# Elementwise work on on-chip data moves from GpSimd to VectorE and ScalarE in a two-block trunk kernel

## The chip, the cores and the metric

The kernel runs on one core of one Trainium2 chip. The metric is device time in microseconds (us). Engines go by the profile's names: PE is TensorE (PEld its weight load), DVE is VectorE, ACT is ScalarE, POOL is GpSimd, SP is SyncE, which here issues most DMAs.

## The reference, cut to what matters

Two blocks run one after the other over 512 latent tokens of 1024 features (the first block also over 256 context tokens). Everything is float32.

```python
# first block, twice: modulation, then three mixers side by side, then a squared-ReLU MLP
u = (rmsnorm(x, g_mix) * (1 + sc1) + sh1) @ w_in            # 1024 -> 2048 and some
mix = concat([pool_mixer(p), gla_output(gla_bidir(...)), latent_attention(q, k, v)]) @ w_out
x = x + ga1 * mix
x = x + ga2 * (square(relu(h @ w_up)) @ w_down)             # hidden width 4096
# second block, once: two recurrent scans side by side, gated and merged, then the same kind of MLP
u = (rmsnorm(x) * (1 + sc) + sh) @ w_in2                     # 1024 -> 14400
conv = silu(causal_depthwise_conv(u_part, w))                # 4 taps
y_gdn = gated_delta_rule(...)                                # 16 heads of 128
y_ssm = ssd_chunked_scan(...)                                # 32 heads of 64, state 128, chunks of 128
merged = sigmoid(g1) * (y_gdn_gated @ w_up1) + sigmoid(g2) * (y_ssm_gated @ w_up2)
x = x + norm(merged @ w_out2);  x = x + norm(mlp(...))
```

## The kernel before

**Products.** Every dense product is done with three float32r matmuls, `mm3`: an operand is split into a high part (rounded to float32r) and a low part (the rest), and high times high, high times low and low times high are added in PSUM. Weights come from DRAM in loads of 128 x 1024, "halves" in what follows: 512 rows and 256 columns. `whalf` (L274 to L287) loads one on SP's queue (L281, three buffers), makes the high part on ACT (L282, two buffers) and the low part by a subtraction that DVE and POOL share: `share` eighths of the columns on DVE (L284), the others on POOL (L285). `share` is 5, so 640 and 384 columns, and 4 between the scans and the merge, so 512 and 512. There are 503 halves. `dense` gives feature-major outputs of 512 tokens (48 matmuls for a half), `tokens` token-major ones (both halves of a group are needed until its end).

**What sets the order.** A scheduler orders the instructions of each engine when the kernel is built, from a simulated timeline; tiles and semaphores are placed by it. `urgent` pulls a weight's load and split and the use of its products ahead. Each engine then takes its instructions strictly in that order.

**First block.** `squares`, `root`, `spread` and `modulate` are the normalisation: squares on ACT, partial sums of them (L378) in turns on DVE and POOL, the power -0.5 of a few columns on POOL (L395). `gla_states` and `gla_out` are the gated linear attention: for each chunk of 128 tokens and each of seven levels, a difference E (L705, POOL), two exponentials (L706, L707, ACT), K (L708, DVE) and Q (L711 POOL, or L726 and L729: a memset on POOL, then half of the partitions on DVE and half on POOL), a product on PE and a masked copy (L734, DVE). `attend` is the softmax attention; its queries are scaled (L912) and turned (L836) on POOL. `mlp` squares the ReLU on POOL (L1051) between two ACT instructions (L1050, L259).

**Second block.** `conv_silu` takes a product's 512 columns: copy (L1283), last tap (L1285 or L1287) and first tap (L1288) on ACT, two taps on DVE (L1291), the first tap added on POOL (L1292), tanh on ACT, the last product on DVE (L1294). `gdn_prep`, `gdn_solve`, `gdn_join` and `gdn_chunk` are the delta rule, four chunks one behind the other; `ssm_chunk` is a chunk of a group of the state space scan (8 groups of 4 chunks), each with steps on PE, ACT, DVE and POOL. The dense products of `silu_tokens` and `sigmoid_gate` come behind the scans in the program, and the scheduler puts them between the scans' steps. `up` merges: its four parts need `gdn_gate` (two parts) and `ssm_gate` (two parts), whose first product is on POOL (L1779, L1800); L1830, L1832 and L1833 apply the gates. `post_norm` (L1260, L1261) adds the normalised output, every second block on POOL; it is the kernel's last step, before the stores.

Of the kernel before, what the change touches and what calls it, by code (L numbers as in the profile page):

```python
# [27 lines left out]
# ---------------------------------------------------------------- host side: layout and shape constants  # L28
# [43 lines left out]
def _bands():  # L72
    """Windowed mean minus the token itself, as matrices over [token in, token out]."""
# [118 lines left out]
# ---------------------------------------------------------------- the kernel  # L192
class Kern:
    SHARED = {"const", "wraw", "whi", "wlo", "mod", "gs", "nv", "nr"} | {f"V{i}" for i in range(8)}
    # work space: tag -> count, of [128, 512]
    WORK1 = dict(E=2, K=2, Q=2, AT=1, QE=1, q=2, d=1, ab=1)
    WORK2 = dict(fa=3, fr=2, fu=2, fy=2, gG=3, gk=2, gm=2, dv=2, dk=2, dq=2, da=2, dn=2, dd=2, jy=2)
    # the tags of a normalisation's square, variance, root and product
# [5 lines left out]
    def __init__(self, ctx, tc, A, at):  # L204
# [3 lines left out]
        self.share = 5  # L208
# [11 lines left out]
    def w(self, tag, n=512, dt=F32):  # L220
        """Work space [128, n]."""
# [21 lines left out]
    # -- small helpers  # L243
# [29 lines left out]
    # -- weights  # L273
    def whalf(self, name, i, n, kb, soon=True):  # L274
        """One load of a packed weight: its two float32r parts, [128, kb, n / kb]."""
# [23 lines left out]
    def dense(self, name, groups, h, n, consume, halves=(0, 1), soon=True):  # L299
        """out^T [128 features, n tokens] per block of 128 columns of the weight; h per block of its rows."""  # L300
# [15 lines left out]
    def tokens(self, name, g, h, ntb, consume):  # L316
        """out [128 tokens, 256] for pairs of token blocks."""
# [39 lines left out]
    def squares(self, x, n, tags, gains=None):  # L357
        """Means over the features of the squares of x, plus epsilon: token-major columns [128, n / 128]. With gains
        [128, 8, 2], as second columns the means of the squares times those."""
# [10 lines left out]
        for k in range(8):  # L370
# [6 lines left out]
            elif k > 1:  # L377
                (nc.gpsimd if k % 2 else nc.vector).tensor_tensor(accs[k % 2], accs[k % 2], sq, op=ALU.add)  # L378
# [8 lines left out]
        # EPS v + mean: the second norm's variance over the first one's factor  # L387
# [4 lines left out]
    def root(self, v):  # L392
        """v ** -0.5"""
# [4 lines left out]
    def spread(self, r):  # L398
        """Columns [128 tokens, blocks] as a row over all partitions, [128, tokens]."""
# [7 lines left out]
    def norm_mod(self, x, n, gs, sh, hs, tags):  # L407
        """hs: pairs that take the two parts of the normalised blocks."""
# [60 lines left out]
    def flush(self):  # L469
        """Ends the pieces that were begun."""  # L470
# [3 lines left out]
    def modulation_v(self, name, st, bias, part, first=0):  # L474
        """The same for the first condition alone, by the vector engine."""
# [20 lines left out]
    def tick(self, n=1):  # L496
        """Does the next pieces of what was left for later."""
# [6 lines left out]
    def gain(self, mod, j, g):  # L504
        """(1 + scale) * gain for condition j."""
# [17 lines left out]
    def after(self, a, tile):  # L523
        """Has the loads into a tile wait for an array: they would take the place of more urgent ones."""
# [1395 lines left out]
```

## Time and profile before

| | |
|---|---|
| three runs, median (lowest to highest) | 3656.49 us (3649.99 to 3657.73) |
| span of the profiled execution | 3646.2 us |
| PE busy, share | 3414.7 us, 94% |
| PE weight load | 2833.3 us, 78% |
| DVE busy, share | 2174.3 us, 60% |
| ACT busy, share | 1466.0 us, 40% |
| POOL busy, share | 1601.3 us, 44% (1370 instructions) |
| mean granted TensorE clock | 0.956 |
| DMA queues, of 16 engines | 38.3% and 3.5% |

The profiled execution's span is 10.3 us under the median of the runs: what lies around the span. A group of the page's costliest instructions gives its busy time, the mean of one, the idle time of the engine before them and what ended it. Ends of matmuls are modelled, so that PE counts as busy while a short matmul's result is still on its way.

### The profile page before, as it was taken

To read this page: it belongs to the slowest core of one execution; us is meant where nothing else is said; L and a number is where in the kernel's file an instruction comes from. 1 tells how busy PE (TensorE), PEld (TensorE's weight loads), DVE (VectorE), ACT (ScalarE), POOL (GpSimd) and SP (SyncE) were. 2 spreads that over 40 slices of the span, in tenths; PEclk is the share of its full clock that TensorE was granted. 3 is DMA by queue.
4 is the path that set the end of the run, shared out by engine and by line. 5 is a ranking of instruction groups with operands and counts; after the bars stand their busy time and mean duration, and the time that the engine had idled before them with its cause. 6 is when DMAs were issued, how large, how long until landed. Compare 5 with 4: busy or idle time off the path is not lost. (4 is left out here: it accounts for less than half of the span.)

```text
span 3646.2 us, 55656 instructions
## 1 busy us (share of the span) xinstructions
PE 3414.7 (94%) x20714; PEld 2833.3 (78%) x20714; DVE 2174.3 (60%) x3724; ACT 1466.0 (40%) x2587; POOL 1601.3 (44%) x1370
## 2 busy tenths in 40 slices
PE   7999999989999999999999998998899998989998
PEld 5777788877788787677788776787898776788886
DVE  4844877457533358755633789768757767564233
ACT  4522765453222255632223655554233323254222
POOL 2522465542343235422344555446445545555433
PEclk9898999999999999999999999999999999989999
DMA  6344124635522220045522364456366666454222
GB/s 224 116 143 137 44 74 140 213 117 162 174 99 98 94 70 22 10 134 189 188 95 91 120 195 131 153 159 191 124 186 203 196 201 184 144 167 145 94 97 75
DMA packets 268414, 492.67 MB, mean 135 GB/s; under 512 B 44912, under 2 KB 129904, under 8 KB 267888
## 3 DMA queue, kind: packets, MB, share of 16 engines
q1 hardware_dynamic: 214128, 447.17, 38.3%
q10 hardware_dynamic: 54016, 41.95, 3.5%
q8 instruction: 163, 2.67, 0.3%
q14 instruction: 107, 0.88, 0.1%
HBM read 431.22 MB, written 57.80 MB: 134 GB/s over the span
## 5 line engine op out<-in xcount | busy, mean ns | idle before, releaser
L285 POOL TENSOR_TENSOR wlo<-wraw,whi 128x384 fp32r<-128x384 f32 (+1 forms) x503 | 736.1, 1464 | 1265.2 <-ACT whi L282 1178.0
L295 PE MATMUL mm<-h,whi 128*128 128x512 f32 (+1 forms) x2344 | 865.3, 372 | 38.1 <-ACT h L418 7.4
L282 ACT ACTIVATE whi<-wraw 128x1024 fp32r<-128x1024 f32 x503 | 530.9, 1056 | 866.2 <-PE mm L296 648.2
L296 PE MATMUL mm<-h,whi 128*128 128x512 f32 (+1 forms) x2344 | 857.6, 366 | 14.2 <-DVE h L419 11.7
L284 DVE TENSOR_TENSOR wlo<-wraw,whi 128x640 fp32r<-128x640 f32 (+1 forms) x503 | 481.7, 958 | 636.3 <-ACT whi L282 629.8
L297 PE MATMUL mm<-h,wlo 128*128 128x512 f32 (+1 forms) x2344 | 841.0, 365 | 6.0 <-DVE wlo L284 5.9
L295 PEld LDWEIGHTS mm<-h,whi 128*128 128x128 f32 x2344 | 448.7, 192 | 124.2 <-ACT whi L282 11.5
L296 PEld LDWEIGHTS mm<-h,whi 128*128 128x128 f32 x2344 | 449.8, 192 | 93.4 <-DVE h L419 20.9
L297 PEld LDWEIGHTS mm<-h,wlo 128*128 128x128 f32 x2344 | 448.4, 192 | 80.7 <-DVE wlo L284 8.8
L296 PE MATMUL mm<-wlo,h 128*128 128x256 f32 x1200 | 353.5, 296 | 32.5 <-DVE wlo L284 27.7
L295 PE MATMUL mm<-whi,h 128*128 128x256 f32 x1200 | 353.2, 297 | 10.7 <-ACT whi L282 9.8
L297 PE MATMUL mm<-whi,h 128*128 128x256 f32 x1200 | 350.0, 293 | 0.0
L296 PEld LDWEIGHTS mm<-wlo,h 128*128 128x128 f32 x1200 | 235.2, 196 | 43.1 <-DVE wlo L284 32.5
L295 PEld LDWEIGHTS mm<-whi,h 128*128 128x128 f32 x1200 | 234.7, 197 | 27.7 <-ACT whi L282 12.5
L297 PEld LDWEIGHTS mm<-whi,h 128*128 128x128 f32 x1200 | 235.2, 196 | 17.2 <-issue 13.7
L295 PE MATMUL mm<-U,whi 128*128 128x512 f32 (+1 forms) x608 | 228.6, 379 | 5.8 <-DVE V L1080 5.8
L296 PE MATMUL mm<-U,whi 128*128 128x512 f32 (+1 forms) x608 | 227.5, 376 | 0.9 <-DVE U L260 0.9
L297 PE MATMUL mm<-U,wlo 128*128 128x512 f32 (+1 forms) x608 | 223.6, 376 | 0.0
L487 DVE SCALAR_TENSOR_TENSOR AT<-mraw,cst,AT 128x512 f32<-128x512 f32 x140 | 119.2, 851 | 88.6 <-DMA mraw<-in_w_ada 52.7
L295 PE MATMUL mm<-big,whi 128*128 128x512 f32 x384 | 155.0, 405 | 5.6 <-ACT whi L282 2.3
L296 PE MATMUL mm<-big,whi 128*128 128x512 f32 x384 | 153.6, 400 | 0.0
L297 PE MATMUL mm<-big,wlo 128*128 128x512 f32 x384 | 150.9, 401 | 0.0
(580 smaller groups left out, 5980.3 us busy)
## 6 DMA issues: line engine op xcount, KB each, us to landing
wraw<-in_w_in SPq DMA_DIRECT2D x166, 512.0 KB, 3.5
wraw<-in_w_up SPq DMA_DIRECT2D x96, 512.0 KB, 3.3
wraw<-in_w_down SPq DMA_DIRECT2D x96, 512.0 KB, 3.3
mraw<-in_w_mod SPq DMA_DIRECT2D x96, 256.0 KB, 3.0
mraw<-in_w_ada SPq DMA_DIRECT2D x96, 256.0 KB, 2.8
wraw<-in_w_out SPq DMA_DIRECT2D x40, 512.0 KB, 3.3
wraw<-in_w_mlp_up SPq DMA_DIRECT2D x40, 512.0 KB, 3.3
mraw<-in_w_late SPq DMA_DIRECT2D x64, 256.0 KB, 2.8
```

Of the source, the lines that this page charges most:

```text
L282: nc.scalar.activation(hi, raw, AF.Copy)
L284: nc.vector.tensor_tensor(lo[:, :c], raw[:, :c], hi[:, :c].bitcast(F32), op=ALU.subtract)
L285: nc.gpsimd.tensor_tensor(lo[:, c:], raw[:, c:], hi[:, c:].bitcast(F32), op=ALU.subtract)
L295: nc.tensor.matmul(out, lh, rh, start=start, stop=False)
L296: nc.tensor.matmul(out, lh, rl, start=False, stop=False)
L297: nc.tensor.matmul(out, ll, rh, start=False, stop=stop)
L487: nc.vector.scalar_tensor_tensor(acc, raw, st[:, k, 0:1], acc, op0=ALU.mult, op1=ALU.add)
```

## The change

- `whalf`: the low part is one DVE subtraction of 1024 columns; `share` is gone.
- `squares`, `gla_states`, `gla_out`, `turn`, the queries' scale, `first_norms`, `post_norm`, `ssm_chunk`, `ssm_gate`, `up`: the POOL instruction becomes a DVE one.
- `mlp`: the square is done by ACT.
- `conv_silu`: the first tap is a third DVE multiply-add; its ACT product and POOL addition are gone.
- `gdn_prep`: the two half subtractions become one DVE instruction of 512 columns; `gdn_chunk`: values are scaled by two ACT instructions, the two decays by one DVE instruction.
- `silu_tokens`: with a gain, ACT's halving and POOL's product become one DVE product with a gain that has been halved once.
- `ssm_chunk`: subtract and clip, two instructions of 512 columns, become four of 128 with both operations.
- `gdn_gate`: POOL's product and two DVE scalings become two DVE instructions.

POOL keeps the roots (L395, 15 of them), its memsets and its copies that hold back loads (L525): 107 rows in its order, where there were 1335. Comments are gone, and line numbers of the changed kernel are up to 7 lower.

```diff
 whalf:
-            c = (n * self.share // 8) // 64 * 64
-            nc.vector.tensor_tensor(lo[:, :c], raw[:, :c], hi[:, :c].bitcast(F32), op=ALU.subtract)
-            nc.gpsimd.tensor_tensor(lo[:, c:], raw[:, c:], hi[:, c:].bitcast(F32), op=ALU.subtract)
+            nc.vector.tensor_tensor(lo, raw, hi.bitcast(F32), op=ALU.subtract)
 squares:
-                (nc.gpsimd if k % 2 else nc.vector).tensor_tensor(accs[k % 2], accs[k % 2], sq, op=ALU.add)
+                nc.vector.tensor_tensor(accs[k % 2], accs[k % 2], sq, op=ALU.add)
 gla_out:
-                nc.gpsimd.tensor_tensor(v(E), v(B), v(B)[:, :, s:s + 1].to_broadcast([128, G, 2 * s]), op=ALU.subtract)
+                nc.vector.tensor_tensor(v(E), v(B), v(B)[:, :, s:s + 1].to_broadcast([128, G, 2 * s]), op=ALU.subtract)
-                    eng = nc.vector if half == f else nc.gpsimd
-                    eng.tensor_tensor(v(Q)[half, :, part], v(qd)[half, :, part], v(E)[half, :, part], op=ALU.mult)
+                    nc.vector.tensor_tensor(v(Q)[half, :, part], v(qd)[half, :, part], v(E)[half, :, part], op=ALU.mult)
 mlp:
-                nc.gpsimd.tensor_tensor(r, r, r, op=ALU.mult)
+                nc.scalar.activation(r, r, AF.Square)
 post_norm:
-            (nc.gpsimd if k % 2 else nc.vector).tensor_tensor(x[k], x[k], y[k], op=ALU.add)
+            nc.vector.tensor_tensor(x[k], x[k], y[k], op=ALU.add)
 conv_silu:
-        nc.scalar.activation(u[:, 3:], raw[:, :NL - 3], AF.Copy, scale=w(0))
-        for j in (2, 1):
+        for j in (2, 1, 0):
             d = 3 - j
             nc.vector.scalar_tensor_tensor(acc[:, d:], raw[:, :NL - d], w(j), acc[:, d:], op0=ALU.mult, op1=ALU.add)
-        nc.gpsimd.tensor_tensor(acc[:, 3:], acc[:, 3:], u[:, 3:], op=ALU.add)
 gdn_chunk:
-            nc.gpsimd.tensor_tensor(v4, v4, self.irk[:, c, hg * 2:hg * 2 + 2].unsqueeze(2).to_broadcast([128, 2, 256]),
-                                    op=ALU.mult)
+            for j in range(2):
+                vj = v[:, j * 256:(j + 1) * 256]
+                nc.scalar.activation(vj, vj, AF.Copy, scale=self.irk[:, c, hg * 2 + j:hg * 2 + j + 1])
 ssm_chunk:
-        nc.vector.tensor_tensor(A4, A4, self.cumS[:, c, hs].unsqueeze(2).to_broadcast([128, 4, 128]), op=ALU.subtract)
-        nc.vector.tensor_scalar(Ab, Ab, 0.0, None, op0=ALU.min)
+        for j in range(4):
+            nc.vector.tensor_scalar(A4[:, j], A4[:, j], self.cumS[:, c, g * 4 + j:g * 4 + j + 1], 0.0,
+                                    op0=ALU.subtract, op1=ALU.min)
-        nc.gpsimd.tensor_tensor(e4(xd), e4(xx), bc(self.dt[:, c, hs]), op=ALU.mult)
+        nc.vector.tensor_tensor(e4(xd), e4(xx), bc(self.dt[:, c, hs]), op=ALU.mult)
 gdn_gate:
-                nc.gpsimd.tensor_tensor(o, o, z, op=ALU.mult)
                 for j in range(2):
-                    nc.vector.tensor_scalar(o[:, j * 128:(j + 1) * 128], o[:, j * 128:(j + 1) * 128],
-                                            self.ors[:, c, hp + j:hp + j + 1], None, op0=ALU.mult)
+                    nc.vector.scalar_tensor_tensor(o[:, j * 128:(j + 1) * 128], o[:, j * 128:(j + 1) * 128],
+                                                   self.ors[:, c, hp + j:hp + j + 1], z[:, j * 128:(j + 1) * 128],
+                                                   op0=ALU.mult, op1=ALU.mult)
```

The order moves with it. DVE's queue where `up` begins, before: the low part of the 393rd half, `wlo_27588`, stands 22 rows behind that of the 392nd (the `gn` rows are a root by Newton's steps for `ssm_gate`).

```order
L1807 SCALAR_TENSOR_TENSOR da_27328<-da_27328,gn_4394_27320,dv_27317 128x256
L1807 SCALAR_TENSOR_TENSOR dn_27334<-dn_27334,gn_4394_27320,dv_27317 128x256
L1743 TENSOR_TENSOR ns_3966_24038<-se_24050,const_69 128x128
L1807 SCALAR_TENSOR_TENSOR dd_27340<-dd_27340,gn_4394_27320,dv_27317 128x256
L1766 TENSOR_TENSOR V_2888_17855<-V_2888_17855,se_24027 128x256
L1744 TENSOR_TENSOR gG_24036<-gG_24036,ns_3966_24038 128x512
L284 TENSOR_TENSOR wlo_27588<-wraw_27586,whi_27587 128x640
L1803 TENSOR_SCALAR gn_4407_27378<-gn_4407_27378 128x4
```

DVE's queue at the same place now: the low part of a half there is `wlo_27177` (L282 of the changed kernel), and the one ahead of it, `wlo_27137`, stands 126 rows further up.

```order
L259 TENSOR_TENSOR big_26863<-gp_26909,big_26863 128x512
L1744 TENSOR_TENSOR gm_23570<-ns_3942_23547,rows_2858_17511 128x256
L1728 TENSOR_TENSOR ssl_23589<-ssl_23589,cum_17553 128x4
L1731 TENSOR_SCALAR gG_23582<-gG_23582,cum_17553 128x128 x4
L259 TENSOR_TENSOR big_26864<-gp_26967,big_26864 128x512
L1794 TENSOR_TENSOR da_26996<-da_26996,dk_26997 128x256
L1739 TENSOR_TENSOR svN_23617<-svN_23617,sp_17527 128x256
L1738 TENSOR_TENSOR gG_23508<-gG_23508,svP_23510 128x512
L1794 TENSOR_TENSOR dn_27002<-dn_27002,dk_27003 128x256
L282 TENSOR_TENSOR wlo_27177<-wraw_27175,whi_27176 128x1024
```

Between two low parts there now stand 125 rows of both scans' last steps and gates, where the largest number near it was 33.

PE's queue at the first system product of the delta rule's third chunk (`gp<-dv,big`), before: it stands behind 9396 of the 13608 dense matmuls, in the products of the half `whi_24861`.

```order
L296 MATMUL mm_24874<-wlo_24862,h_2836_17670 128x256
L297 MATMUL mm_24874<-whi_24861,h_2836_17670 128x256
L1597 MATMUL gp_20924<-dv_20903,big_20467 128x128 x4
L295 MATMUL mm_24874<-whi_24868,h_2837_17671 128x256
L295 MATMUL mm_24930<-whi_24861,h_2836_17670 128x256
```

PE's queue at the same product now: it stands behind 9911 dense matmuls, five groups of weights further on.

```order
L292 MATMUL mm_25112<-whi_25101,h_2836_17400 128x256
L1589 MATMUL gp_20577<-dv_20556,big_20128 128x128 x2
L293 MATMUL mm_25112<-wlo_25102,h_2836_17400 128x256
L1589 MATMUL gp_20577<-dv_20556,big_20128 128x128 x2
L294 MATMUL mm_25112<-whi_25101,h_2836_17400 128x256
```

The steps of both scans have moved back against the dense products by some 250 to 500 matmuls, while the dense products keep their own order.

## Rows read from the trace of the kernel before

**Rows 1.** Span with granted clock; then busy time, share, instructions of each engine.

```profile
core 0: 3646.2 us, clock 0.956
...
PE 3414.7 (94%) x20714; PEld 2833.3 (78%) x20714; DVE 2174.3 (60%) x3724; ACT 1466.0 (40%) x2587; POOL 1601.3 (44%) x1370
```

**Rows 2.** Stages: us, busy PE, PEld, DVE, ACT, POOL (instructions), PEclk, DMA, GB/s.

```profile
417.00:661.00 244.00, 237.70 (x2053) 198.98 (x2052) 184.81 (x363) 134.53 (x319) 138.66 (x132) 0.99 0.32 104
...
1336.00:1570.00 234.00, 217.25 (x1684) 169.94 (x1684) 174.13 (x358) 134.65 (x340) 108.49 (x103) 0.91 0.09 28
...
2144.00:3045.00 901.00, 822.72 (x5360) 705.48 (x5359) 678.87 (x1180) 360.47 (x586) 467.98 (x431) 0.96 0.56 173
...
3304.00:3605.00 301.00, 301.00 (x1332) 244.78 (x1332) 89.97 (x106) 93.50 (x124) 123.88 (x85) 1.00 0.30 100
```

**Rows 3.** What PE waited for, whole span: us in total, times, longest.

```profile
PE mm L296 <- DVE wlo L284: 27.7, 19, 3.9
...
PE mm L296 <- DVE h L419: 11.7, 15, 1.6
PE sm L1303 <- DVE fa L1294: 8.8, 5, 3.4
...
PE mm L295 <- ACT h L418: 7.4, 6, 2.6
...
PE mm L296 <- POOL wlo L285: 4.7, 5, 2.5
```

**Rows 4.** Timeline of DVE and POOL in the first MLP: start us, duration us.

```profile
1014.26 0.83 DVE L284 TENSOR_TENSOR wlo<-wraw,whi 128x640 fp32r<-128x640 f32 x1 [4.21 <-ACT whi L282]
...
1014.36 1.60 POOL L285 TENSOR_TENSOR wlo<-wraw,whi 128x384 fp32r<-128x384 f32 x1 [1.53 <-ACT whi L282]
...
1015.00 1.51 DVE L260 TENSOR_TENSOR U<-Q,U 128x512 fp32r<-128x512 f32 x1
...
1018.11 0.69 DVE L260 TENSOR_TENSOR U<-Q,U 128x512 fp32r<-128x512 f32 x1 [1.59 <-ACT U L259]
```

**Rows 5.** Groups by form, whole span: busy us, mean ns, idle before.

```profile
L1292 POOL TENSOR_TENSOR fa<-fa,fu 128x509 f32<-128x509 f32 x64 | 99.8, 1560 | 115.7 <-DVE fa L1291 58.4 <-issue 12.8 <-ACT fy L250 8.7
...
L284 DVE TENSOR_TENSOR wlo<-wraw,whi 128x640 fp32r<-128x640 f32 x454 | 433.0, 954 | 618.1 <-ACT whi L282 614.0 <-POOL gG L378 1.3 <-PE gp L1604 1.2
...
L1294 DVE SCALAR_TENSOR_TENSOR fa<-fu,fa 128x512 f32<-128x512 f32 x64 | 57.2, 894 | 15.6 <-ACT fu L1293 15.2
L1291 DVE SCALAR_TENSOR_TENSOR fa<-fr,const,fa 128x510 f32<-128x510 f32 x64 | 53.8, 840 | 1.1
...
L1050 ACT ACTIVATE Q<-mm 128x512 f32<-128x512 f32 x64 | 37.6, 587 | 45.2 <-PE mm L297 45.2
```

**Rows 6.** The start of `up`: one stage as in rows 2, then DVE's timeline.

```profile
3045.00:3067.00 22.00, 20.53 (x101) 16.44 (x99) 17.54 (x43) 7.81 (x20) 12.02 (x14) 1.00 0.62 181
...
3046.15 0.16 DVE L270 SCALAR_TENSOR_TENSOR gn<-gn,gn 128x4 f32<-128x4 f32 x1
...
3053.48 0.68 DVE L1832 TENSOR_TENSOR fa<-mm,fa 128x512 f32<-128x512 f32 x1
...
3054.15 0.41 DVE L1755 TENSOR_TENSOR gm<-se,ea 128x256 f32<-128x256 f32 x1
...
3060.32 0.48 DVE L1807 SCALAR_TENSOR_TENSOR dq<-dq,gn,dv 128x256 f32<-128x256 f32 x1
3060.72 0.48 DVE L1807 SCALAR_TENSOR_TENSOR da<-da,gn,dv 128x256 f32<-128x256 f32 x1
```

**Rows 7.** Timeline of DVE and POOL at the kernel's end.

```profile
3633.58 1.41 DVE L1260 SCALAR_TENSOR_TENSOR dv<-dv,gs,gp 128x512 f32<-128x512 f32 x2 [2.35 <-PE gp L403]
...
3641.72 0.68 DVE L1261 TENSOR_TENSOR V<-V,dn 128x512 f32<-128x512 f32 x1
```

More of the change, by code (lines that the diff above doesn't have):

```diff
@@ L207, in __init__ @@
         self.flip = self.flop = 0
-        self.share = 5
         self.later, self.folds, self.spare, self.rate = [], [], [], 1
@@ L642, in sums @@
             nc.scalar.activation(d, tot, AF.Exp)
-            nc.gpsimd.tensor_tensor(B[64:], B[64:], y[64:], op=ALU.subtract)
+            nc.vector.tensor_tensor(B[64:], B[64:], y[64:], op=ALU.subtract)
             dec.append(d)
@@ L709, in gla_out @@
                 if lv >= 5:
-                    nc.gpsimd.tensor_tensor(Q, qd, E, op=ALU.mult)
+                    nc.vector.tensor_tensor(Q, qd, E, op=ALU.mult)
                     if X is None:
@@ L835, in turn @@
                                     sin[:, :, xx].unsqueeze(1).to_broadcast([128, nh, 2, 16]), op=ALU.mult)
-        nc.gpsimd.tensor_tensor(dst, two(hv(a)), two(hv(b)), op=ALU.add)
+        nc.vector.tensor_tensor(dst, two(hv(a)), two(hv(b)), op=ALU.add)
     def keys(self, l, o, n, table):
@@ L911, in queries @@
             c = (g * ntb + qb) * 4
-            nc.gpsimd.tensor_tensor(a4, a4, sc[:, c:c + 4].unsqueeze(2).to_broadcast([128, 4, 64]), op=ALU.mult)
+            nc.vector.tensor_tensor(a4, a4, sc[:, c:c + 4].unsqueeze(2).to_broadcast([128, 4, 64]), op=ALU.mult)
             d = self.w("d")
@@ L1251, in first_norms @@
                 nc.scalar.activation(xs[k], xs[k], AF.Copy, scale=g[:, k:k + 1])
-                nc.gpsimd.tensor_tensor(xs[k], xs[k], p, op=ALU.mult)
+                nc.vector.tensor_tensor(xs[k], xs[k], p, op=ALU.mult)
     def post_norm(self, y, x, gw, n):
@@ L1372, in small_heads @@
         self.copy(cols.rearrange("p a c e -> p (a c e)"), lp[:, :192], "v")
-        self.cumG, self.loc, self.tail = cols[:, 0], cols[:, 1], cols[:, 2]
+        self.cumG, self.near, self.tail = cols[:, 0], cols[:, 1:3], cols[:, 2]
         tS, tG = self.sm(), self.ps("gp", 3)
@@ L1456, in gdn_prep @@
             nc.sync.dma_start(kq, self.qkf[:, c, hg * 2:hg * 2 + 2])
-            for a, col in ((slice(0, 64), self.loc), (slice(64, 128), self.tail)):
-                nc.gpsimd.tensor_tensor(G4[:, :, a], G4[:, :, a],
-                                        col[:, c, hg * 4:hg * 4 + 4].unsqueeze(2).to_broadcast([128, 4, 64]),
-                                        op=ALU.subtract)
+            G5 = Gb.rearrange("p (h a t) -> p h a t", h=4, a=2)
+            near = self.near[:, :, c, hg * 4:hg * 4 + 4].rearrange("p a h -> p h a")
+            nc.vector.tensor_tensor(G5, G5, near.unsqueeze(3).to_broadcast([128, 4, 2, 64]), op=ALU.subtract)
             nc.vector.tensor_scalar(Gb, Gb, 0.0, None, op0=ALU.min)
@@ L1476, in gdn_prep @@
             e4 = Gb.rearrange("p (j r t) -> p j r t", j=2, r=2)
-            nc.gpsimd.tensor_tensor(e4, e4, g3[:, :, 1].unsqueeze(2).to_broadcast([128, 2, 2, 128]), op=ALU.mult)
+            nc.vector.tensor_tensor(e4, e4, g3[:, :, 1].unsqueeze(2).to_broadcast([128, 2, 2, 128]), op=ALU.mult)
             nc.sync.dma_start(self.atd[c][:, hg * 512:(hg + 1) * 512], Gb)
@@ L1584, in gdn_chunk @@
                 nc.scalar.activation(qe, qe, AF.Exp)
-                for j in range(2):
-                    q3 = p4(qe)[:, 2 * j:2 * j + 2]
-                    nc.gpsimd.tensor_tensor(q3, q3, kq[:, j, 1].unsqueeze(1).to_broadcast([128, 2, 128]), op=ALU.mult)
+                q4 = qe.rearrange("p (j r t) -> p j r t", j=2, r=2)
+                nc.vector.tensor_tensor(q4, q4, kq[:, :, 1].unsqueeze(2).to_broadcast([128, 2, 2, 128]), op=ALU.mult)
                 ks = gp()
@@ L1665, in f @@
                 hz, th = self.w("fa"), self.w("fr")
-                nc.scalar.activation(hz, ps, AF.Copy, scale=0.5)
                 nc.scalar.activation(th, ps, AF.Tanh, scale=0.5)
+                if gain is None:
+                    nc.scalar.activation(hz, ps, AF.Copy, scale=0.5)
+                else:
+                    j4 = lambda a: a.rearrange("p (j e) -> p j e", j=4)
+                    nc.vector.tensor_tensor(j4(hz), j4(ps), gain.unsqueeze(1).to_broadcast([128, 4, 128]), op=ALU.mult)
                 nc.vector.scalar_tensor_tensor(hz, th, 1.0, hz, op0=ALU.add, op1=ALU.mult)
-                if gain is not None:
-                    z4 = hz.rearrange("p (j e) -> p j e", j=4)
-                    nc.gpsimd.tensor_tensor(z4, z4, gain.unsqueeze(1).to_broadcast([128, 4, 128]), op=ALU.mult)
                 nc.scalar.dma_start(dst[b:b + 2, :, g * 256:(g + 1) * 256].rearrange("c p e -> p c e"),
@@ L1749, in ssm_chunk @@
         t, u = y[:, :256], y[:, 256:]
-        nc.gpsimd.tensor_tensor(e4(u), e4(xx), bc(self.Drow[:, hs]), op=ALU.mult)
+        nc.vector.tensor_tensor(e4(u), e4(xx), bc(self.Drow[:, hs]), op=ALU.mult)
         nc.vector.tensor_tensor(t, u, yp[:, :256], op=ALU.add)
@@ L1755, in ssm_chunk @@
             nc.vector.tensor_tensor(e4(u), e4(yo[:, :256]), bc(ea[:, c, hs]), op=ALU.mult)
-            nc.gpsimd.tensor_tensor(t, t, u, op=ALU.add)
+            nc.vector.tensor_tensor(t, t, u, op=ALU.add)
         nc.scalar.dma_start(self.yd[c][:, g * 256:(g + 1) * 256], t)
         if c < 3:
-            nc.gpsimd.tensor_tensor(e4(xd), e4(xd), bc(sm[:, 1]), op=ALU.mult)
+            nc.vector.tensor_tensor(e4(xd), e4(xd), bc(sm[:, 1]), op=ALU.mult)
             up = yo[:, 256:]
@@ L1764, in ssm_chunk @@
             else:
-                nc.gpsimd.tensor_tensor(e4(Sg), e4(Sg), bc(sm[:, 0]), op=ALU.mult)
+                nc.vector.tensor_tensor(e4(Sg), e4(Sg), bc(sm[:, 0]), op=ALU.mult)
                 nc.vector.tensor_tensor(Sg, Sg, up[:, :256], op=ALU.add)
@@ L1799, in ssm_gate @@
                 nc.sync.dma_start(z, zd[c][:, g * 256:(g + 1) * 256])
-                nc.gpsimd.tensor_tensor(y[:, :256], y[:, :256], z, op=ALU.mult)
+                nc.vector.tensor_tensor(y[:, :256], y[:, :256], z, op=ALU.mult)
                 nc.scalar.activation(y[:, 256:], y[:, :256], AF.Square, accum_out=ss[:, c:c + 1])
@@ L1832, in f @@
                     nc.vector.tensor_tensor(s, ps, s, op=ALU.mult)
-                    nc.gpsimd.tensor_tensor(merged[m], merged[m], s, op=ALU.add)
+                    nc.vector.tensor_tensor(merged[m], merged[m], s, op=ALU.add)
             self.dense(("w_gdn_up2", "w_ssm_up2")[i // 2], range(i % 2 * 4, i % 2 * 4 + 4), parts[i], NL, f)
@@ L1854, in block2 @@
         self.ssm(h, space[4:])
-        self.share = 4
+        nc.vector.tensor_scalar(self.gnw, self.gnw, 0.5, None, op0=ALU.mult)
         zg, zs = self.dram([4, 128, 2048], "zg"), self.dram([4, 128, 2048], "zs")
@@ L1862, in block2 @@
         merged = self.blocks()
-        self.share = 5
         self.up(zg, zs, gd, gs, merged)
```

1 line of the change is left out of this document (removed).

## The prediction

> **What bounds the kernel now.** I read the engines' totals first. PE is busy for 3414.7 of 3646.2 us, so 231.5 us of the span are PE's idle time; DVE has 60%, POOL 44%, ACT 40% [rows 1]. [...] The totals hide stages with different limits, so the stage table comes next [rows 2]. In the last MLP, 3304 to 3605, PE is busy for the whole 301.0 us at full clock while POOL is busy for 123.88: nothing that POOL does there holds PE up, and taking it away can save nothing. In the scan stage, 2144 to 3045, PE is idle for 901 - 822.72 = 78.3 us, a third of all its idle time, and DVE is at 678.87 of 901, 75%. Two short stages of the first block are as tight for DVE: 417 to 661 with 76% and 1336 to 1570 with 74%. These three stages decide.
>
> The waits of PE then say what it waits for [rows 3]. No single wait is large. Low parts of weights come first: 27.7 us in 19 waits put down to DVE's share, 4.7 in 5 put down to POOL's. Then the normalised input (11.7 and 7.4) and the end of the convolution (8.8).
>
> Why a low part is late can be read in one place of the first MLP [rows 4]. DVE's 640 columns start at 1014.26 and take 0.83, POOL's 384 start at 1014.36 and end at 1015.96, so the pair is ready 1.70 us after its start. Beside POOL's instruction a DVE subtraction of 512 columns takes 1.51; with POOL idle the same instruction takes 0.69. So the two engines hold each other up, and DVE's busy time contains waiting: over the kernel its 640 columns take 0.954 in the mean [rows 5] against 0.83 alone, 15% more.
>
> **The change, part by part.**
>
> *Low parts.* One DVE instruction of 1024 columns. The trace has none; 512 columns take 0.69 and 640 take 0.83 [rows 4], 0.14 for 128 columns, so 0.83 + 3 x 0.14 = 1.25. The part is ready 1.70 - 1.25 = 0.45 us earlier than now. The 24 waits of [rows 3] shrink by that much each: **gain 11**, between 0 (DVE's queue is fuller, so that it starts later) and the 32.4 that stand there.
>
> *Chains that lose a POOL step or a wait for POOL.* In the convolution the two taps and the POOL addition take 0.840 each and 1.560, the last product 0.894 [rows 5]: 4.13 us. Now three taps and the last product, each about 0.75 without POOL beside it: 3.0, over a quarter less. The normalisation loses its POOL additions. Taking a third off the three waits of [rows 3] (27.9 us) is a **gain of 9**, bounds 0 and 20.
>
> *Steps that stand later in PE's order.* PE meets the scans' steps 250 to 500 dense matmuls later, while the dense order is the same. At 0.226 us for one (301.0 / 1332, [rows 2]) a step has 55 to 115 us more until PE comes to it. DVE is also fuller there, so the step itself comes later. Of the scan stage's idle 78.3, less 11 that are counted above, I take a quarter: **gain 16**, bounds 0 and 65; the other sign is the first rival.
>
> *The clock.* The clock is lower in the stages with idle PE (0.91 in 1336 to 1570 where PE idles 7% of the time, 1.00 in 3304 to 3605, [rows 2]). [...]
>
> *The clump before `up`.* DVE's order now has 125 rows, 146 instructions, between the low part of the 392nd half and that of the 393rd. By their widths: 36 of 4 columns at 0.16, 16 of 512 at 0.68, 56 of 256 at 0.41 to 0.48, 38 of 128 at about 0.28 (an estimate between the 4 and the 256) [rows 6]; 5.8 + 10.9 + 23.5 + 10.6 = 51 us. Successive instructions overlap (two of 0.48 start 0.40 apart, [rows 6]), which takes off up to 146 x 0.08 = 12; I take 42. PE can only go on with what has been split: one half of 48 products at 0.226, 10.8 us, or two, 21.7. The rest, 42 - 16 = 26, is idle time that isn't there now: PE is busy for 20.53 of the 22 us from 3045 [rows 6]. **Cost 26**, from 0 (if DVE has run ahead of PE and does these rows early) to 42 - 10.8 = 31, and 40 without overlap.
>
> *The kernel's end.* From 3633.58 to 3642.40 DVE does eight scalings (pairs of 1.41) and four additions, POOL four additions beside it [rows 7]. Now DVE does 8 x 0.70 + 8 x 0.68 = 11.0 us, less overlap, against 8.8: **cost 2**.
>
> *DVE's tight stages of the first block*, 417 to 661 and 1336 to 1570: POOL's 138.66 and 108.49 us come to queues at 76% and 74%. POOL's columns cost DVE 0.69 / 1.56 = 0.44 of POOL's time (512 columns on DVE alone [rows 4], 509 on POOL [rows 5]), and its waits of about 13% of its present time vanish: 184.81 + 61 - 24 = 222 of 244, 91%, and 174.13 + 48 - 23 = 199 of 234, 85%. Bounds: 0, because the work beside is not needed at once, and 25 (a tenth of one stage). **Cost 5**, nearer to 0, since DVE's share may grow where its present idle time is mostly waiting for a weight's high part.
>
> *At nothing:* the MLP's square on ACT. A 512-column ACT instruction there takes 0.587 [rows 5], and ACT is busy for 93.50 of 301 us in the last MLP [rows 2], so 64 more of them hide under PE; if that cover went, 64 x 0.587 = 38 us would be bare over both blocks' MLPs. The values scaled on ACT and the gain folded into the halving go with it: ACT at 40% has room. POOL's remaining 107 rows have no one waiting on them more than now.
>
> Sum: 11 + 9 + 16 + 12 - 26 - 2 - 5 = 15. The profiled span becomes 3646.2 - 15 = 3631, and with the 10.3 us by which the median of the runs is longer, **3641 us**.
>
> **The rivals.**
>
> *DVE becomes the bound in the scan stage (slower).* POOL's 467.98 us there cost DVE 0.44 x 468 = 206; the waits that vanish are 13% of 679, 88; taps, clips and scalings that go take some 15. So 679 + 206 - 88 - 15 = 782 of 901, 87% [rows 2]. DVE takes its instructions strictly in order, and many of its steps wait for PE, ACT or a DMA; the highest share that this kernel shows over a long stage is 76%, with PE at 97% beside it. If 82% is what such a queue can keep up, the stage lasts 782 / 0.82 = 954, 53 more. With the clump (26), the end and the first block's stages (7), less the gains of low parts and chains (20), and with neither later placement nor clock to gain, that is 3646.2 + 66 + 10.3 = about 3722; with half of the clump, 3709. The point from which it decides is the share at which DVE's work fills the present stage, 87%: a queue that can keep more costs nothing here. For it: the scheduler itself put the scans' steps later and left a clump at `up`. Against it: steps that lose POOL lose a hand-over too, and the waits of DVE become fewer. [...]
>
> *Much more is gained.* The waiting beside POOL touches every chain of the kernel. [...] Against it: PE's waits are spread over forty kinds, most without POOL in them. [...]
>
> *Nothing moves.* PE is at 94%, POOL is not named in its larger waits but for 4.7 us, and what the low parts gain the clump takes: 20 - 26 - 2 = -8, or 0.2%: 3656 to 3665.
>
> *The change doesn't do what it says.* POOL keeps roots, memsets and copies: 107 rows. But none of its 1335 rows of elementwise work on weights or activations is left but the 15 roots, so this has next to no chance.
>
> **How the numbers follow.** My forecast has 0.42, the much larger gain 0.14, nothing 0.12, DVE as the bound 0.32. About 0.2% (7 us, 3649 to 3664) is what a measurement of this kernel can tell from no change. The forecast's own range is 3612 to 3662 (gains down by 20, or costs down to their lower ends), so a fifth of it falls into "no change"; a little of the "nothing" falls on the slower side. Faster: 0.34 + 0.14 = 0.48. Same: 0.08 + 0.10 = 0.18. Slower: 0.32 + 0.02 = 0.34. The range for 8 in 10 goes from 3570, inside the large gain, to 3709.
>
> **What would show each step.** Low parts: a group of 1024 columns with a mean near 1.25, and fewer PE waits on it. Chains: the third tap near 0.75, PE's waits for the convolution and the normalised input down by a third. POOL: busy for well under 100 us, and DVE's 512-column instructions near 0.69 everywhere. Later placement: PE's idle time in the scan stage at 52 to 62 us instead of 78.3. Clump: a gap of PE of some 26 us ahead of the 393rd half's low part. Clock: above 0.956 in the mean. First block: unchanged lengths of its two tight stages. The forecast is wrong if DVE's share in the scan stage stays near 82% while the stage grows, if the gap at `up` is missing or twice as long, or if 1024 columns take much more than 1.25.

## The result, and the profile after

The changed kernel takes 3592.69 us (median of 4 runs, 3591.49 to 3593.71) against 3657.11 for the kernel before: a ratio of 0.9834, 95% interval 0.9814 to 0.9854. That is 1.7% faster, four times what was forecast, and inside the stated range only because that range reached into the case "much more is gained". Runs of the kernel before spread over some 30 us (3639 to 3670 in the comparisons below), those of the changed kernel over 10, and the profiled execution of before was one of its quicker ones.

The totals of the changed kernel, span and clock first, to be read against [rows 1]:

```profile
core 0: 3590.1 us, clock 0.957
...
PE 3392.4 (94%) x20714; PEld 2823.2 (79%) x20714; DVE 2238.5 (62%) x4339; ACT 1517.7 (42%) x2675; POOL 58.5 (2%) x105
```

POOL went from 1601.3 to 58.5 us, and DVE grew by only 64 us. PE is idle for 197.7 us where it was 231.5; its busy time fell by 22.3. The granted clock hardly moved (0.957 for 0.956).

Stages of the changed kernel, with the columns of [rows 2]. They are cut where the changed kernel reaches the same dense products as the kernel before at 424, 661, 1336, 1570, 2144, 3160, 3304 and 3605 us, so that the stages hold the same products. First two rows of the kernel before that [rows 2] doesn't have, from 424 to 661 and over scans and `up` together:

```profile
424.00:661.00 237.00, 230.70 (x2011) 193.56 (x2010) 178.66 (x351) 130.75 (x309) 134.65 (x130) 1.00 0.33 107
...
2144.00:3160.00 1016.00, 929.75 (x5829) 791.17 (x5828) 755.37 (x1325) 394.81 (x656) 529.16 (x486) 0.96 0.56 173
```

Then the changed kernel:

```profile
418.00:665.00 247.00, 237.52 (x2057) 200.98 (x2058) 194.12 (x425) 140.29 (x338) 11.09 (x22) 0.97 0.32 103
...
1330.00:1558.00 228.00, 212.51 (x1679) 166.88 (x1679) 180.91 (x430) 134.51 (x339) 10.51 (x20) 0.93 0.10 30
...
2921.00:2966.00 45.00, 25.90 (x81) 17.42 (x80) 32.98 (x117) 11.16 (x31) 0.00 (x0) 0.54 0.57 175
...
3247.00:3548.00 301.00, 301.00 (x1330) 244.76 (x1329) 100.22 (x106) 112.84 (x152) 0.00 (x0) 1.00 0.30 98
...
2124.00:3109.00 985.00, 919.52 (x5831) 785.67 (x5830) 764.75 (x1673) 375.23 (x625) 10.42 (x9) 0.96 0.57 178
```

Scans and `up` went from 1016 to 985 us: 31 of the 56 us. The first block ends at 2124 where it was 2144, which is 20, all of it behind 665 us (up to there the changed kernel is 4 us later); the stretch from the end of `up` to the last MLP gave 6; the last MLP is unchanged at 301.0 us with PE busy all the time. DVE does 764.75 us of work in the scans and `up` where it did 755.37, although POOL's 529.16 us there came down to 10.42.

What PE waited for (us in all, times, longest). [rows 3] lacks one row of low parts in the kernel before:

```profile
PE mm L297 <- DVE wlo L284: 5.9, 4, 2.9
```

The changed kernel, against [rows 3] and this row:

```profile
PE mm L293 <- DVE wlo L282: 16.3, 15, 2.3
PE gp L1777 <- DVE dv L1774: 10.9, 5, 3.9
PE mm L293 <- DVE h L416: 9.8, 11, 2.9
PE mm L292 <- ACT whi L281: 9.0, 8, 4.5
...
PE mm L292 <- ACT h L415: 7.0, 6, 2.5
...
PE mm L294 <- DVE wlo L282: 3.9, 3, 1.8
```

The waits put down to low parts fell from 38.3 us (27.7 + 4.7 + 5.9) to 20.2, those for the normalised input from 19.1 to 16.8. This list doesn't hold the gain: it names who came last, and most of the 56 us isn't in any of its larger rows.

The DVE groups tell more (busy us, mean ns, idle before). First the kernel before, then the changed one, for two kinds of instruction: `U<-Q,U` has both operands in on-chip memory, `V<-mm,mod,V` takes one from PSUM:

```profile
L260 DVE TENSOR_TENSOR U<-Q,U 128x512 fp32r<-128x512 f32 x64 | 63.1, 987 | 37.4 <-ACT U L259 37.2
...
L1080 DVE SCALAR_TENSOR_TENSOR V<-mm,mod,V 128x512 f32<-128x512 f32 x80 | 59.5, 749 | 62.5 <-PE mm L297 62.1
```

```profile
L282 DVE TENSOR_TENSOR wlo<-wraw,whi 128x1024 fp32r<-128x1024 f32 x502 | 613.5, 1222 | 513.6 <-ACT whi L281 509.2 <-DMA bt<-fy 0.9 <-PE mm L294 0.5
...
L1076 DVE SCALAR_TENSOR_TENSOR V<-mm,mod,V 128x512 f32<-128x512 f32 x80 | 59.4, 748 | 53.8 <-PE mm L294 53.1
...
L1286 DVE SCALAR_TENSOR_TENSOR fa<-fr,const,fa 128x510 f32<-128x510 f32 x64 | 47.9, 749 | 0.7
...
L1288 DVE SCALAR_TENSOR_TENSOR fa<-fu,fa 128x512 f32<-128x512 f32 x64 | 44.1, 689 | 4.7 <-ACT fu L1287 4.5
L259 DVE TENSOR_TENSOR U<-Q,U 128x512 fp32r<-128x512 f32 x64 | 44.0, 690 | 73.9 <-ACT U L258 73.9
```

The first kind fell from 987 to 690 ns; the second was 749 and is 748. Two edits act on the first here: the low parts leave POOL, and so does the MLP's square, which ran beside `U<-Q,U`. The low part of 1024 columns takes 1222, the taps 749 where they took 840, the convolution's last product 689 where it took 894 [rows 5].

### The profile page after: what moved, and what is told of

The parts are those of the page before. It is cut to its first block, busy times and chain, and to the rows that moved or that the text cites. A ratio compares the mean times of both kernels' runs of the same rounds, so it can differ in the third digit from the quotient of the medians.

```text
span 3590.1 us, 53732 instructions
## 1 busy us (share of the span) xinstructions
PE 3392.4 (94%) x20714; PEld 2823.2 (79%) x20714; DVE 2238.5 (62%) x4339; ACT 1517.7 (42%) x2675; POOL 58.5 (2%) x105
## 4 chain that ended last, share of the span: by engine, by line
PE 62%; issue 12%; DVE 11%; DMA 10%; ACT 3%; SPq 1%; POOL 0%; DVEq 0%; POOLq 0%; ACTq 0%
PE mm L292 15%; PE mm L293 15%; PE mm L294 15%; DMA mraw<-in_w_ada 2%; DVE wlo L282 2%; PE op L952 2%; PE sm L729 1%; DMA mraw<-in_w_late 1%; PE SC L447 1%; DVE AT L484 1%; DMA gG<-rowS 1%; PE SL L926 1%; ACT whi L281 1%; PE mm L590 1%; DVE svP L1498 1%
## 5 line engine op out<-in xcount | busy, mean ns | idle before, releaser
L282 DVE TENSOR_TENSOR wlo<-wraw,whi 128x1024 fp32r<-128x1024 f32 x503 | 614.2, 1221 | 519.2 <-ACT whi L281 514.9
L292 PE MATMUL mm<-whi,h 128*128 128x256 f32 x1200 | 348.3, 293 | 10.9 <-ACT whi L281 7.8
L294 PE MATMUL mm<-whi,h 128*128 128x256 f32 x1200 | 343.9, 288 | 0.0
L484 DVE SCALAR_TENSOR_TENSOR AT<-mraw,cst,AT 128x512 f32<-128x512 f32 x140 | 104.9, 750 | 96.7 <-DMA mraw<-in_w_ada 58.4
L1286 DVE SCALAR_TENSOR_TENSOR fa<-fr,const,fa 128x511 f32<-128x511 f32 (+2 forms) x192 | 142.5, 750 | 26.0 <-ACT fa L1281 13.4
```

The source lines that it names most:

```text
L282: nc.vector.tensor_tensor(lo, raw, hi.bitcast(F32), op=ALU.subtract)
L292: nc.tensor.matmul(out, lh, rh, start=start, stop=False)
L294: nc.tensor.matmul(out, ll, rh, start=False, stop=stop)
L484: nc.vector.scalar_tensor_tensor(acc, raw, st[:, k, 0:1], acc, op0=ALU.mult, op1=ALU.add)
L1286: nc.vector.scalar_tensor_tensor(acc[:, d:], raw[:, :NL - d], w(j), acc[:, d:], op0=ALU.mult, op1=ALU.add)
```

## The experiments

In this section "alone" means the kernel before with one part of the change, and "undone" the changed kernel without one part. All medians are in us, all ratios are to the kernel before on the same chip.

### Four parts, each alone

The low parts (`e_w_alone`): the change's edit of `whalf`, and nothing else.

> The kernel before with one edit: the low part of each weight half is one DVE subtraction of 1024 columns, everything else stays on GpSimd. Waiting theory (what the change gains is the time that DVE and POOL hold each other up, and the hand-over between them, in every stage): 15 to 25 us faster, the 1024-column group at 1.22 to 1.30 us in the mean because POOL's other work is still beside it, PE's waits for low parts down from 38.3 to some 25 us. Placement theory (the gain comes from scan steps that stand later in PE's order): 0 to 8 us faster, since they stand only some 100 dense matmuls later here. Load theory (DVE's fuller queue costs): slower by 0 to 10 us.

The other three take over whole functions of the changed kernel:

```diff
+ e_scan_alone:  conv_silu, small_heads, gdn_prep, gdn_chunk, ssm_chunk
+ e_first_alone: squares, gla_states, gla_out, turn, attend, mlp, first_norms
+ e_gates_alone: silu_tokens, gdn_gate, ssm_gate, up, post_norm
```

> The kernel before with the edits of the convolution, gdn_prep, gdn_chunk and ssm_chunk; weights' low parts, the first block and the gates as before. Waiting theory: 20 to 35 us faster, all of it between the start of the second block and the end of up, nothing before 2144 us. Placement theory: some 10 to 15 us, since the steps stand 100 to 200 dense matmuls later and not 250 to 500. Load theory: 0 to 10 us slower.

> The kernel before with the edits of the first block and the MLPs' square (squares, gla_states, gla_out, turn, the queries' scale, mlp, first_norms). Waiting theory: 5 to 12 us faster, all before 2144 us. Placement theory: nothing, 0 to 3 us. Load theory: 0 to 5 us slower in the two stages where DVE is at 75%.

> The kernel before with the edits of silu_tokens, gdn_gate, ssm_gate, up and post_norm. Waiting theory: 0 to 6 us faster, between 2650 us and the end of up, and 1 us slower at the kernel's end. Placement theory: 0 to 4 us. Load theory: 0 to 5 us slower.

| part alone | median | ratio, 95% interval |
|---|---|---|
| low parts | 3608.22 | 0.9862, 0.9841 to 0.9883 |
| scans and convolution | 3652.18 | 0.9995, 0.9981 to 1.0009 |
| first block and MLPs | 3644.05 | 0.9967, 0.9954 to 0.9980 |
| gates, `up`, closing norms | 3645.54 | 0.9979, 0.9963 to 0.9994 |

One edit of three lines carries most of the gain: 1.4%, 45 us by the medians and 50 by the ratio. It gained twice what the waiting theory allowed it, while the scans' part, to which that theory gave 20 to 35 us, gained nothing that can be measured; this also speaks against the placement theory, since the scans' steps do stand some 100 to 200 dense matmuls later there. The first block gave 0.33%, 9 to 12 us, the top of what was expected of it, and the gates 8, where the waiting theory had 0 to 6.

And these 45 to 50 us are not in PE's waits for low parts. In this run they are still

```profile
PE mm L294 <- DVE wlo L283: 25.3, 20, 3.1
...
PE mm L295 <- DVE wlo L283: 8.4, 8, 2.0
```

33.7 us, against 38.3 in the kernel before. Something else becomes faster when POOL leaves the low parts alone. PE's whole idle time is 211.6 us (a span of 3609.0 less 3397.4 busy), 20 less than before, and the granted clock is higher: 0.9632 in the mean of the five runs against 0.9569 in the 25 of the kernel before on that chip. By the estimate (1 - clock) x time, which takes the whole time to go with the clock and which no run tests, 133 us (0.0368 x 3608.22) are lost to the lower clock instead of 157 (0.0431 x 3653.14).

### Two parts, each undone

```diff
+ e_scan_undone: conv_silu, small_heads, gdn_prep, gdn_chunk, ssm_chunk of the kernel before
+ e_w_undone:    whalf (and the shares) of the kernel before
```

> The changed kernel with the convolution, gdn_prep, gdn_chunk and ssm_chunk as before (small_heads too), so that POOL keeps 253 of its scan instructions. The clump of 125 DVE rows ahead of the 394th low part is gone from the order (37 at most near it). Clump theory (the scans' part gained nothing alone and costs a gap of 45 us without dense products in the whole change): 10 to 25 us faster than the changed kernel, 3568 to 3583. Additive theory (parts add up, the clump cost is made up by what stands elsewhere): 3590 to 3596, as the changed kernel. Waiting theory (scan steps gain from POOL's absence as much as the weights do): 5 to 20 us slower than the changed kernel.

> The changed kernel with the low parts shared between DVE and POOL as before. If the parts add up: 0.9995 x 0.9967 x 0.9979 = 0.994 of before, some 3632 us, 40 slower than the changed kernel. If the waiting beside POOL is what counts, the low parts on POOL hold up more DVE work now than before, and it is at 3640 to 3655.

Without the scans' part: 3599.69, ratio 0.9852 (0.9833 to 0.9872). The median is 7 us above the changed kernel's, and the intervals overlap. Its order has no clump at `up`, and it is no faster for it: the clump theory falls. Between the other two this run does not decide; 7 us lie at the lower end of the waiting theory's 5 to 20, and the noise leaves room for the additive theory's nothing. Without the low parts' edit: 3611.88, ratio 0.9894 (0.9876 to 0.9912). Both expectations missed it, 3632 if the parts add up and 3640 to 3655 by the waiting. So the low parts are worth 45 to 50 us when done first and some 20 when done last, and the other parts 1.1% together without them though only 0.6% when each is done alone. The parts do not add up; why is not shown.

### POOL put back, with nobody waiting for it

The changed kernel again, with a POOL instruction behind each low part. It writes into the raw half, which is dead by then.

```diff
 whalf (e_pool384; e_pool768 with 768 columns):
             nc.vector.tensor_tensor(lo, raw, hi.bitcast(F32), op=ALU.subtract)
+            m = min(n, 384)
+            nc.gpsimd.tensor_tensor(raw[:, :m], raw[:, :m], hi[:, :m].bitcast(F32), op=ALU.subtract)
 whalf (e_poolset):
+            nc.gpsimd.memset(raw, 0.0)
+            nc.gpsimd.memset(raw, 0.0)
+            nc.gpsimd.tensor_tensor(raw[:, :64], raw[:, :64], hi[:, :64].bitcast(F32), op=ALU.subtract)
```

> The changed kernel plus one POOL subtraction of 384 columns for each weight half, written into the raw half when DVE has read it; nobody uses what it writes, and only the next load into that buffer waits for it. POOL is busy for some 60 + 700 us again, and the weights are ready as early as in the changed kernel. Port theory (what the low parts' move gained is DVE's and ACT's other steps no longer held up beside POOL): 20 to 45 us slower than the changed kernel, DVE's 512-column instructions at 0.75 to 0.9 us in the mean where they were near 0.69. Readiness theory (the gain is that one engine makes the low part with nothing to wait for): 0 to 8 us slower.

> The same with 768 columns, POOL busy for some 60 + 1250 us. Port theory: about twice the loss of the run with 384 columns, 40 to 80 us slower than the changed kernel. Readiness theory: 0 to 15 us slower.

> The changed kernel plus, for each weight half and at the same place as in the run with 768 columns, two POOL memsets of the raw half (1024 columns each, they write and read nothing) and a POOL subtraction of 64 columns that reads both parts. POOL is busy for about as long as with 768 columns (some 60 + 1000 us) and keeps the raw half and the high part for as long, but reads almost nothing. Port theory (what holds DVE up is a POOL instruction that reads on-chip data beside a DVE instruction with two such operands): 0 to 15 us slower than the changed kernel, DVE's rows as short as there but for the small subtraction. Holding theory (the loss with 768 columns came from buffers kept too long, or from POOL being busy at all): 80 to 150 us slower, as with 768 columns.

> The changed kernel itself, as the measure for the run beside it, on the same chip: 3585 to 3600 us, ratio to before 0.982 to 0.986.

What the expectations call the port theory is that DVE's steps are held up beside POOL's reading; what in the hardware holds them up no run shows. In the table the first and the last row were taken on one chip, the two between on another.

| changed kernel with | POOL busy | median | ratio, 95% interval |
|---|---|---|---|
| nothing (beside its own memsets and roots) | 58.8 | 3590.85 | 0.9837, 0.9815 to 0.9859 |
| 384 columns subtracted | 647.6 | 3614.72 | 0.9902, 0.9875 to 0.9929 |
| 768 columns subtracted | 1060.2 | 3741.20 | 1.0248, 1.0226 to 1.0270 |
| two memsets, 64 columns | 1257.0 | 3612.65 | 0.9888, 0.9865 to 0.9911 |

With 768 columns the kernel is 149 us slower than the changed kernel's 3592.69, with 384 it is 22; that is far more than twice as much, and slower than before: more than the port theory asked for. With 384 `U<-Q,U` has 856 ns in the mean, inside the expected 0.75 to 0.9 us. The memsets keep POOL busy for longer and cost 22 us, above the 0 to 15 expected, far from the 149. The DVE groups show why. With 768 columns:

```profile
L259 DVE TENSOR_TENSOR U<-Q,U 128x512 fp32r<-128x512 f32 x64 | 80.5, 1258 | 65.4 <-ACT U L258 65.4
...
L1078 DVE SCALAR_TENSOR_TENSOR V<-mm,mod,V 128x512 f32<-128x512 f32 x80 | 59.5, 747 | 53.1 <-PE mm L296 52.9
```

and with the memsets, whose own POOL group stands last:

```profile
L1079 DVE SCALAR_TENSOR_TENSOR V<-mm,mod,V 128x512 f32<-128x512 f32 x80 | 59.9, 749 | 59.5 <-PE mm L297 59.0
...
L259 DVE TENSOR_TENSOR U<-Q,U 128x512 fp32r<-128x512 f32 x64 | 44.9, 704 | 63.9 <-ACT U L258 63.9
...
L283 POOL MEMSET wraw<- 128x1024 f32 x502 | 480.8, 958 | 1908.9 <-DVE wlo L282 1899.7 <-ACT E L653 7.1 <-DVE nv L383 1.6
```

With POOL's subtraction of 768 columns, which reads, the DVE instruction with two on-chip operands went from 690 to 1258 ns in the mean; with the two memsets, which only write, and the 64 columns it stayed at 704; the one with an operand in PSUM stayed at 747 to 749 in both kernels and in the five runs with POOL put back.

Scans and `up`, stage rows of the run with 768 columns and of the one with memsets:

```profile
2187.70:3234.10 1046.40, 939.05 (x5831) 793.60 (x5830) 888.07 (x1674) 374.64 (x628) 265.58 (x131) 0.95 0.54 168
```

```profile
2139.00:3122.40 983.40, 920.98 (x5831) 787.59 (x5830) 778.38 (x1673) 376.34 (x625) 309.57 (x370) 0.96 0.57 179
```

With 768 columns the stage takes 61 us more than the changed kernel's 985; the rest of the 149 lies outside it. The memsets cost nothing here: 983.4 against 985 us. Their 22 us lie elsewhere, by the profiled executions 15 before 2139 us and 7 after `up`. The granted clock is lower with them, 0.9530 in the mean of the five runs against 0.9572 in the five of the changed kernel on that chip, by the same estimate 170 us lost instead of 154. That the raw halves which they hold meet the loads there is argued, not shown, and it makes the 22 us of the run with 384 columns no clean price of the reading.

### Is it POOL's queue, or POOL's reading?

A low part on POOL does two things: it stands in POOL's queue ahead of other steps, and it reads. These two runs start from the low parts alone on DVE (3608) and put one of the two back, or both.

```diff
 whalf (e_w_set):
             nc.vector.tensor_tensor(lo, raw, hi.bitcast(F32), op=ALU.subtract)
+            nc.gpsimd.memset(raw, 0.0)
+            nc.gpsimd.memset(raw[:, :n // 2], 0.0)
 whalf (e_w_port):
+            nc.gpsimd.tensor_tensor(raw[:, :384], raw[:, :384], hi[:, :384].bitcast(F32), op=ALU.subtract)
```

> The run with the low parts alone on DVE (3608 us, 0.986 of before), plus two POOL memsets for each weight half (1024 and 512 columns, about 1.5 us together, as long as the 384-column subtraction that POOL did there), put into the raw half when DVE has read it. [...] Queue theory (the low parts' move gained because POOL's other steps no longer stand behind low parts in POOL's queue): back to 3635 to 3655. Port theory (it gained because DVE's rows are no longer held up by POOL's reading): 3605 to 3620.

> The run with the low parts alone on DVE, plus one POOL subtraction of 384 columns for each weight half into the raw half when DVE has read it, so that POOL reads as much as in the kernel before, in the same queue, but no product waits for it. Port theory: 3645 to 3675, as before or slower. Queue theory: the same as with the memsets, 3635 to 3655. If the gain was that products no longer wait for POOL's part of the low part (hand-over), both runs stay at 3605 to 3620.

Memsets: 3613.23, ratio 0.9884 (0.9852 to 0.9915). Subtraction: 3638.76, ratio 0.9949 (0.9931 to 0.9968), under the port theory's 3645 to 3675. Span and totals of both, then the stage row of scans and `up`, memsets first:

```profile
core 0: 3609.6 us, clock 0.956
...
PE 3405.2 (94%) x20714; PEld 2830.0 (78%) x20714; DVE 2246.3 (62%) x3724; ACT 1469.6 (41%) x2587; POOL 1627.3 (45%) x1873
...
2137.60:3125.50 987.90, 917.31 (x5826) 783.32 (x5825) 762.25 (x1325) 395.74 (x656) 539.43 (x605) 0.97 0.57 178
```

```profile
core 0: 3643.2 us, clock 0.960
...
PE 3405.4 (93%) x20714; PEld 2822.5 (77%) x20714; DVE 2364.4 (65%) x3724; ACT 1468.1 (40%) x2587; POOL 1456.4 (40%) x1370
...
2135.20:3155.30 1020.10, 927.40 (x5831) 786.79 (x5831) 795.36 (x1326) 395.26 (x657) 511.13 (x485) 0.97 0.55 172
```

In the stage POOL is busy for 539 us in the one and 511 in the other. The stage is 32 us longer in the one whose POOL reads, and DVE is busy for 33 us more. Over the whole kernel DVE is busy for 118 us more, and PE is idle for 33 us more (237.8 against 204.4) at the same busy time. The queue theory falls: memsets in the queue cost nothing here, and 5 us over the kernel, inside the intervals. The subtraction also keeps the high part in use, which the memsets do not; but ACT, which writes the next one, waits for that subtraction only twice, 5.4 us in all. So reading costs 25 to 31 us (3638.76 against 3613.23 and 3608.22), short of the full 45 to 50.

What the other 18 us are (3656.75 to 3638.76, on one chip) is open. A product needs no POOL part any more even in the run whose POOL reads, but that doesn't show as less waiting. PE's waits for low parts in that run are

```profile
PE mm L295 <- DVE wlo L283: 29.4, 22, 4.4
PE mm L296 <- DVE wlo L283: 18.5, 14, 2.6
```

47.9 us where the kernel before has 38.3; PE is idle for 237.8 us where it was 231.5, and scans and `up` take 1020.1 where they took 1016. What differs is the granted clock: 0.9613 in the mean of the eleven runs against 0.9535 in the fifteen of the kernel before on that chip, by the same estimate 141 us lost instead of 170, more than the 18. Why it is higher no run shows.

Two DVE groups of these runs, `U<-Q,U` with the memsets and with the subtraction, show the reading on one instruction:

```profile
L260 DVE TENSOR_TENSOR U<-Q,U 128x512 fp32r<-128x512 f32 x64 | 62.1, 974 | 7.1 <-ACT U L259 6.9
```

```profile
L260 DVE TENSOR_TENSOR U<-Q,U 128x512 fp32r<-128x512 f32 x64 | 75.8, 1184 | 12.0 <-ACT U L259 11.3
```

(974 and not 690, since the MLP's square is still on POOL in both. In the trace of the memsets 42 of the 64 have no POOL instruction that reads beside them and take 687 ns in the mean, the other 22 take 1520.)

## Why the prediction was wrong

The direction was right and the mechanism was seen: [rows 4] was read as two engines that hold each other up. The sum was wrong by a factor of four, 15 us against 56 in the profiled spans and 64 in the medians. By its own steps:

- **Low parts, gain 11, bounds 0 and 32.4: the step that failed.** Their duration was right (1.25 forecast, 1.222 measured). The term was sized by PE's waits that the profile puts down to low parts, 24 of them at 0.45 us each. (The 0.45 came from one place, where POOL took 1.60; its group has 1.458 in the mean. The 0.83 called alone stood beside POOL's instruction there.) Those waits fell by 4.6 us when the edit was made alone, and the kernel by 45 to 50, more than the upper bound. Put in its place by the runs: 25 to 31 us because POOL's reading no longer stretches DVE's steps, which stand in many chains and in no single row of the waits, and 18 us whose cause stays open and which come with a higher granted clock. The 13% of waiting in DVE's rows was known and was used in the prediction only to work out DVE's load. It was never given a term as time gained.
- **Chains, gain 9: right in size as waits.** The three waits went from 27.9 to 16.8 us, 11 less; the taps took 0.749 (0.75 forecast). But the scans' and the convolution's own edits give no time alone, and last no more than 7 us within the noise, so the shorter chain is not shown to be worth the 9.
- **Later placement, gain 16, and the clump, cost 26: both happened, neither paid.** Over scans and `up` PE's idle time fell from 86.3 to 65.5 us. The clump is in the trace: from 2921 to 2966 PE does no dense product, is idle for 45 - 25.9 = 19 us, and the granted clock is 0.54. The prediction said 26. But the run without the clump isn't faster. Nor is the gap what the term took it for, PE waiting for the next split half: PE's longest waits in it are for `dv` (7.0 us) and `gG` (3.7), a low part starts at 2929.89, inside it, and the next one only at 2984.87, when PE has been at dense products again since 2966. (They are the 393rd and the 394th, one later than the prediction counts.) What PE does in that gap are scan steps that otherwise stand between dense products; the dense products had come some 104 us earlier than before by then. Summing a gain and a cost for the two sides of one shift was the error; they should have been one term near zero.
- **Clock, gain 12:** no run shows this term; it was the author's estimate. What the runs show in its place is the granted clock, 0.957 in the profiled execution where it was 0.956; by the estimate (1 - clock) x span that is 154 us (0.043 x 3590.1) against 160 (0.044 x 3646.2), 6 us less. With the low parts' edit alone the same estimate gives 24 us (157 less 133); in the whole change that is not seen.
- **The end, cost 2:** 41.2 us were to become 43; the stage is 42.1. Right.
- **DVE's tight stages, cost 5, at 91% and 85%:** measured 194.12 of 247 and 180.91 of 228, both 79%. The first is longer than the 237 us of the same products before, but 46 matmuls moved into it and its clock is 0.97 for 1.00, some 7 us of PE (237.52 busy for 230.70); up to its end the kernel is 4 us later. The second became 6 us shorter. Together there was no cost.
- **The square on ACT at nothing:** right; the last MLP is at 301.0 us in both, with ACT at 112.84.
- **The rival "DVE becomes the bound"** rested on 782 of 901 us, 87%. Measured over scans and `up`: 764.75 of 985, 78%, after 755.37 of 1016, 74%. The error is the price of 0.44 for each of POOL's microseconds: for the low parts, a large part of POOL's time there, DVE only goes from some 1.0 us for its share to 1.22 for the whole, and the rest is paid for by the waiting that vanishes. With that the rival had no ground, and a third of the chance stood on it.
- **The base:** 10.3 us were added for what lies around the span. In the changed kernel it is 3592.06 - 3590.1 = 2.0. The 10.3 were the distance between a quick execution and the median.

Of the rivals, "much more is gained" was the one that came about, with 64 us by the medians where the forecast had 15, and in part for the reason given there: the waiting beside POOL touches many chains.

What stays open: what the 18 us are, why the parts do not add up, why the memsets cost 22 us outside the scans, and why 768 columns cost nearly seven times as much as 384 and not twice. Of the last the traces show this much: against the changed kernel DVE is busy for 121 us more with 384 columns and for 376 more with 768, and PE's waits for low parts go from 20.2 us to 22.2 and to 47.0.

## What to carry to other kernels

When two engines hold each other up, don't price the removal by the waits that name them; compare the mean of one instruction form with its lone duration over the whole kernel, and give that excess a term of its own wherever the engine's steps feed the bound engine. Move the largest reader on POOL first: here one subtraction, 503 times, was worth 1.4% by itself, and moving some 280 instructions of the scans by itself nothing measurable. Here `U<-Q,U`, with two on-chip operands, kept its lone duration beside memsets, which only write (704 ns for 690 in the mean), and `V<-mm,mod,V`, with an operand in PSUM, kept its own in both kernels and in the five runs with POOL put back (747 to 749). That doesn't make memsets free: two for each half cost the changed kernel 22 us, and the kernel with the low parts alone on DVE 5, inside the intervals.

## What the runs showed of the hardware

One-operand DVE instructions were stretched too, which was not expected. `gG<-gG`, a clip of 512 columns in place, and `ssl<-gG`, a copy of 4 columns, in the kernel before and then in the changed one:

```profile
L1461 DVE TENSOR_SCALAR gG<-gG 128x512 f32<-128x512 f32 x16 | 13.8, 862 | 1.6 <-POOL gG L1458 1.6
...
L1734 DVE COPY ssl<-gG 128x4 f32<-128x4 f32 x32 | 10.5, 328 | 55.7 <-DMA gG<-rowS 55.5 <-POOL ns L1759 0.2
```

```profile
L1454 DVE TENSOR_SCALAR gG<-gG 128x512 f32<-128x512 f32 x16 | 6.7, 418 | 0.0
...
L1727 DVE COPY ssl<-gG 128x4 f32<-128x4 f32 x32 | 5.7, 177 | 45.4 <-DMA gG<-rowS 45.4
```

862 became 418 ns and 328 became 177. With POOL's memsets, which read nothing, these two were longer as well, 513 and 249 ns. In the changed kernel with two memsets behind each low part:

```profile
L1457 DVE TENSOR_SCALAR gG<-gG 128x512 f32<-128x512 f32 x16 | 8.1, 513 | 0.0
...
L1730 DVE COPY ssl<-gG 128x4 f32<-128x4 f32 x32 | 8.0, 249 | 36.9 <-DMA gG<-rowS 36.8
```

In that trace the 25 copies without POOL beside them take 169 ns in the mean, three beside a memset 676. Why these two were longer with the memsets and `U<-Q,U` hardly was (704 ns for 690), no run shows. The second thing is the shape of the loss: with POOL's added reading at 1.17 us for each half the kernel lost 22 us, and at 1.99 us it lost 149.
